# A two-layer trunk on one core: lone turns of the first attention and of the second layer's memory weights move next to other fp32 work, and the last output tile's end goes by halves

## The chip, the cores and the metric

The kernel runs on one core of one Trainium2 chip. Time is device time in microseconds (us) of one execution; a kernel's time is the median over its runs. TensorE (PE in the profile) does the matrix products, ScalarE (ACT) activations and copies with a scale, VectorE (DVE) elementwise work and reductions, GpSimd (POOL) a few fills, and SyncE (SP) issues nearly all DMA transfers.

## The reference

The reference is a trunk of two layers on x [1, 512, 1024] with 256 memory tokens. All values are fp32. Cut to what matters:

```python
def reference(x, mem, ...):
    for i in range(2):
        h = rms_norm(x, attn_norm[i])
        if i == 0:                       # differential attention, 6 heads
            proj = h @ w_in_diff[0]      # q, k, v, mem_q
            mix = diff_attention(q, k, v, ...)
        else:                            # gated linear attention, 4 heads
            proj = h @ w_in_gla[0]       # q, k, v, r, gate_low, mem_q
            mix = gla_attention(q, k, v, r, ...)
        cross = memory_cross_attention(mem_q, mem, ...)   # 4 heads, 256 tokens
        x = x + concatenate([mix, cross], -1) @ w_out[i]
        h = rms_norm(x, ffn_norm[i])
        x = x + conv_ffn(h, w_up[i], conv_w[i], conv_b[i], w_down[i])
    return x

def diff_attention(q, k, v, ...):        # d = 64, two maps m per head
    q = rms_norm(q, g[0]) * d ** -0.5
    k = rms_norm(k, g[1])
    p = softmax(q @ k.T + t5_bias, masked by 64-token chunks)
    w = p[map 0] - lam * p[map 1]
    return rms_norm(w @ v, out_norm_g) * (1 - lam_init)

def conv_ffn(h, w_up, conv_w, conv_b, w_down):            # DFF = 2816
    a, g = split(causal_depthwise_conv3(h @ w_up) + conv_b)
    return (silu(g) * a) @ w_down
```

## The kernel before

**Layout.** The stream x is held transposed, as eight tiles of 128 features by 512 tokens. Each product with a weight is done as three fp32r matmuls on halves of a number: high by high, high by low, low by high (lines 328 to 330 in `gemm`, 349 to 351 in `product`). The weights come in blocks of 512 KB on SyncE's queue into `raw` (three buffers); ScalarE rounds a block to `whi` (L251), VectorE makes the rest `wlo` (L254), and six buffers of each run ahead of TensorE.

**Two kinds of work on TensorE.** Besides the long runs of fp32r matmuls there are short fp32 ones: transposes (L218), logits (L733 in layer 0, L605 for the memory), values (L774, L643) and, in layer 1, the linear attention's products. They depend on ScalarE and VectorE and are strewn into the long runs by hand. A "lone turn" is a group of four transposes that stands alone between fp32r matmuls.

**The order written out by hand.** The strings `SCRIPT` (layer 0) and `GLA` (layer 1) are lists of words. A number takes that many microseconds of units (two contraction tiles of a gemm each) from the queue of fillers `F`; a letter calls a function with the number behind it. The letters of `SCRIPT` that matter here:

- `N` i: `norms`, the group norm of q (even i) or k (odd i) of head pair i // 2. ScalarE squares (L384, two instructions of 128x512), VectorE sums (L385), ScalarE does Ln and Exp (L239, L240), VectorE a Newton step (L225 to L227) and the scaling in place of `qs` or `ks` (L390, 128x1024).
- `P` h: `prepare`, the transposes of head h's `qs` and then `ks` on TensorE, each into a PSUM bank, which ScalarE copies out with a scale (L696).
- `L`, `M` t: `logits` of group t (with the banks lg or tp): matmuls (L733), bias and maximum on VectorE (L740), Exp on ScalarE (L743), weights on VectorE (L748 to L752).
- `T` t: `turn`, the transposes of the weights into a bank tp; ScalarE copies it out (L762).
- `V` t: `values` (L774); behind a head's last group come its Squares on ScalarE (L785).
- `s` h scales a head's output `o`, `F` h: `finish` transposes it and splits it into `xsh` (ScalarE, L308) and `xsl` (VectorE, L309).
- `a`, `b`: operands of the memory's gemms; `X` loads x again; `l`, `t`, `v`: logits, turn and values of the memory attention.

Layer 1's string has its own letters: `t` and `l` as above with `ma.turn` copying on VectorE (L630), `d`, `p`, `s`, `a`, `k`, `S`, `o`, `r`, `G`, `f` for the linear attention, `X` for the loads of x and the start of the output projection.

**What sets the order of the rest.** TensorE runs in the order in which the program calls it. The instructions of ScalarE and VectorE are put into one fixed order per engine when the program is built: a scheduler picks among those that it holds to be ready, by their place in the program, so a letter that moves in a string can move instructions on these engines too. On the chip each engine follows its own list and waits on semaphores of the others.

**PSUM.** Eight banks of 128x512 fp32 in four tags of two: mm (gemms), sm, lg, tp. The next use of a bank waits until its last reader is done.

**The tail.** The last feed-forward part adds a product's bank to two output tiles at a time. For the last one, n = 7, two half adds on VectorE (L1183) are followed each by a DMA to the output, one on SyncE's and one on ScalarE's queue (L1184).

Of the kernel before, what the change touches and what calls it, by code (L numbers as in the profile page):

```python
# [21 lines left out]
S = 512  # L22
# [14 lines left out]
VNAMES = ('v0', 'v0', 'v2')  # L37

SCRIPT = """
    17.75 P0 3.9  # L40
    L0 M1 a3 3.4 P1 5.05 a0 0.97
    1.94 a1 T0
    L2 M3 a2 3.57
    T1 4.86 N2 V0 T2 N3 V1 12.33
    L4 P2 4.55 P3 1.62 V2 T3 2.27 T4
    L5 M6 s0 V3 b1 2.6 V4 1.3 T5 1.3
    L7 M8 3.5 T6 F0 3.64 b0
    V5 T7 8.42 V6 s1 N5 N4 F1
    L9 V7 P4 b2 4.45 T8 T9 s2 3.0
    L10 V8 3.55 X P5 q0  # L50
    L11 b3 V9 T10 4.2
    L12 F2 V10 s3 T11 3.8 q1 k0
# [12 lines left out]
""", """  # L65
    l0 6.85 t0 t3
    l1
    d0 t2 1.55 t1 11.5 t5 14.85 t7 t4 7.15 p0 9.85 k0
    s0
    d1 S0 t6 a0 v0 v1 a1 S1 p1 o0 o1  # L70
    s1 r0 a2 k1
    d2 a3 p2 8.85 S2 0.75 o2 S3 G0 k2 o3 r1
    s2 a4 6.5 a5 S4 2.6 G1 S5
    d3 p3 o4 1.95 f0 0.65 o5 14.95 f1 r2
    s3 f2 a6 G2 1.95 k3 X 3.25 a7 0.65 S6 o6 1.0 f3 S7 o7 r3 13.25 G3 f4 f5
""")
K8 = tuple(range(KT))
C4 = tuple(range(4))
# [100 lines left out]
def trunk(ctx, tc, head_d, x_t, mem_t, wpack, cols_a_d, cols_d, conv_d, gate_d, rel_bias, diff_lambda, consts, onehot, out):  # L179
# [135 lines left out]
    def gemm(sh, sl, nb, key, w, evac, hook=None, late=False, spare=False):  # L315
        got, open_ = [], {}

        piece = [q[0] for q in plan].index(key)

        def unit(b, k0, k1):  # L320
            if not got:
                got.extend(weights(key, True))
            if k0 == 0:
                open_[b] = bank("tp" if spare and b == 0 else "lg" if late and b > 1 else "mm")[:, :w]
            p = open_[b]
            for k in range(k0, k1):
                hi, lo = got[k]
                mm(p, sh[k][:, blk(b)], hi, start=k == 0, stop=False)  # L328
                mm(p, sh[k][:, blk(b)], lo, start=False, stop=False)  # L329
                mm(p, sl[k][:, blk(b)], hi, start=False, stop=k == KT - 1)  # L330
                if b == nb - 1:
                    freed(piece, k)
            if k1 == KT:
                if hook is not None and b == 0:
                    hook()
                evac(b, open_.pop(b))
        units = [(b, k) for b in range(nb) for k in range(0, KT, 2)]
        if late:
            units.sort(key=lambda u: u[0] == nb - 1 or u[1] == KT - 2)
        for b, k in units:  # L340
            F.add(6 * w / 2370.0, lambda b=b, k=k: unit(b, k, k + 2))
# [84 lines left out]
    def token_rsqrt(tag, sq, nb, y, on_dve=False):  # L426
        p, ss = bank(tag), small("ss")[:, :nb]
        for b in range(nb):
            transpose(p[:, blk(b)], sq[:, blk(b)])
        V.reduce_sum(ss, p[:, :128 * nb].rearrange("p (b n) -> p b n", b=nb), axis=AX.X)  # L430
        return rsqrt(ss, nb, 1.0 / D, on_dve, y=y)
# [116 lines left out]
    def mem_kv(l):  # L548
        hs, ls = [None] * KT, [None] * KT
        km = [None]  # L550

        def operands(ks=range(KT)):
            if l == 0 and km[0] is None:
                mem_squares()
            if km[0] is None:
                km[0] = xtile().rearrange("p (b n) -> p b n", b=2)
            for k in ks:
                if k % 2 == 0:
                    mh, ml = split_tiles()
                c = blk(k % 2, 256)  # L560
                hs[k], ls[k] = mh[:, c], ml[:, c]
                split(hs[k], ls[k], memT[k // 2][:, c], c_mem(l, k))

        def ev(b, p):
            A.activation(km[0][:, b], p[:, :256], AF.Copy, scale=r_mem[:, b:b + 1])
            A.activation(vm[l][:, b], p[:, 256:], AF.Copy, scale=r_mem[:, b:b + 1])

        def keys(tag="lg"):
            F.need(f"kv{l}")
            p = bank(tag)  # L570
            for hp in range(2):
                for b in range(2):
                    transpose(p[:, 256 * hp + 128 * b:256 * hp + 128 * b + 128], km[0][:, b, blk(hp)])
            A.activation(kmT[l].rearrange("p a b -> p (a b)"), p, AF.Copy, scale=c_mk(l))
        gemm(hs, ls, 2, ("kv", l), 512, ev,
             (lambda: token_rsqrt("lg", mem_acc[0], 2, r_mem)) if l == 0 else None)
        F.add(0.0, lambda: group_norm(None, km[0], 2, 4, 64))
        F.mark(f"kv{l}")
        return operands, keys


    class MemAttn:
# [38 lines left out]
                V.tensor_mul(pv, pv, rc[:, blk(j, 2)].unsqueeze(2).to_broadcast([128, 2, 256]))  # L621
                self.live[2 * b + j] = pe

        def turn(self, u):
            pe = self.live[u]
            pt = bank("tp")
            for t in range(4):
                transpose(pt[:, blk(t)], pe[:, blk(t)])
            pT = xtile()
            (V.tensor_copy if self.l or u % 2 == 0 else A.copy)(pT, pt)  # L630
            self.live[u] = pT
# [27 lines left out]
    def diff_layer(pool, mix, acc):  # L659
# [28 lines left out]
        def prepare(h):  # L688
            pr, j = divmod(h, 2)
            t2 = []  # L690
            for src, g, nm in zip(qk[pr], (c_dq, c_dk), ("qT", "kT")):
                dst = pool.tile([128, S], F32, name=nm, bufs=3)
                p = bank("tp")
                for b in range(NB):
                    transpose(p[:, blk(b)], src[:, b, blk(j)])
                A.activation(dst, p, AF.Copy, scale=g)  # L696
                t2.append(dst)
            if j == 0:
                pairs[pr] = dict(s2=small("smd").rearrange("p (m b) -> p m b", b=8), nm=small("nmd"), rc=small("rcd"))
            heads[h] = dict(q=t2[0], k=t2[1], v=vs[pr], j=j, left=NB)  # L700
# [113 lines left out]
        for key in ORDER:  # L814
# [19 lines left out]
            "N": lambda i: norms(i // 2, i % 2), "a": lambda i: ops[0]((2 * i, 2 * i + 1)),  # L834
            "b": lambda i: ops[1]((2 * i, 2 * i + 1)), "k": lambda i: keys[i]("sm"),
            "q": lambda i: ma.queries() if i else (F.need("v2"), ma.norm()),
            "l": lambda i: ma.logits(i), "t": ma.turn, "v": lambda i: ma.values(i, "sm"),
            "s": lambda i: scales.pop(i)(), "X": lambda i: load_x(x_t),
            "O": lambda i: last.append(out_proj(0, mix, 1, acc, 5)), "!": lambda i: F.flush()}
        do(SCRIPT, doing)  # L840
# [4 lines left out]
    def gla_layer(pool, mix, acc):  # L845
# [203 lines left out]
        def finish(t):  # L1049
# [9 lines left out]
        do(GLA[1], {  # L1059
            "d": decays, "p": products, "s": scores, "a": lambda i: past_scores(i // 2, i % 2), "k": turn_keys,  # L1060
            "S": lambda i: states(i // 2, i % 2), "o": lambda i: outputs(i // 2, i % 2), "r": norm, "G": gate,
            "f": finish, "X": lambda i: (load_x(xres), out_proj(1, mix, 0, None)), "t": ma.turn, "l": lambda i: ma.logits(2 * i, 2 * i + 1),
            "v": lambda i: ma.values(i)})
        F.flush()

# [44 lines left out]
    def ffn(pool, l, acc):  # L1110
# [36 lines left out]
        for half, nq in enumerate(HALVES):  # L1147
            mids = []
            for q in range(base, base + nq):
                wa = weights(("ua", l, q))  # L1150
                wg = None
                for n in range(2):
                    ua = up(wa, n)
                    wg = wg or weights(("ug", l, q))
                    ug = up(wg, n)
                    if q == 0 and n == 0:
                        row_scales(acc[0])
                    ca = conv(*ua, 2 * q + n)
                    cg = conv(*ug, 22 + 2 * q + n)
                    A.activation(cg, cg, AF.Silu)  # L1160
                    V.tensor_mul(ca, ca, cg)
                    mh, ml = split_tiles() if len(mids) < 5 else split_tiles(pool, "mid", 18)
                    A.copy(mh, ca)
                    V.tensor_sub(ml, ca, mh.bitcast(F32))
                    mids.append((mh, ml))
            last = half == 1
            if last and l == 0:
                tables("natural_log_exp_and_others")
            acc2 = [None]
            for c in range(4):  # L1170
                if last and l == 0 and c == 0:
                    gw = gate_raw[0] = pool.tile([128, S], F32, name="cvo", bufs=6)[:96, :384]
                    G.memset(gw, 0.0)
                    for b in range(3):
                        load(gw[32 * b:32 * b + 17], gate_d)
                pn = bank("lg"), bank("tp")
                parts = weights(("dn", l, base, c))
                for n in range(2):
                    product(pn[n], parts, n, mids)
                for n in range(2):  # L1180
                    if last and l == 1 and c == 3 and n == 1:
                        for t, queue in ((blk(0, S // 2), nc.sync), (blk(1, S // 2), nc.scalar)):
                            V.tensor_add(xT[7][:, t], xT[7][:, t], pn[n][:, t])  # L1183
                            queue.dma_start(out[7, :, t], xT[7][:, t])  # L1184
                        continue
                    update(2 * c + n, pn[n], (lambda k: c_attn(1, k)) if last and l == 0 else None, acc2)
                    if last and l == 0:
                        nc.sync.dma_start(xres[2 * c + n], xT[2 * c + n])
                    if last and l == 1:
                        nc.sync.dma_start(out[2 * c + n], xT[2 * c + n])  # L1190
            base += nq
# [87 lines left out]
```

## Time and profile before

| | us |
|---|---|
| median of 3 runs (1164.59 to 1164.97) | 1164.59 |
| the profiled execution | 1164.66 |
| its span, first to last instruction | 1162.9 |
| TensorE busy, 5648 matmuls | 1158.3 |
| VectorE busy, 1261 instructions | 752.8 |
| ScalarE busy, 951 instructions | 544.9 |

The profile is one execution, taken by the hardware profiler. In a timeline a row gives the start, the length, the engine, the line of the program, the operation, its output and inputs, the shape and how many instructions are joined in the row; behind them may stand the engine's idle time in front of it and who ended it. Matmuls are pipelined: their own length (0.39 for 512 columns) is longer than the step from one to the next, so costs on TensorE are read from start to start. "PEclk" is the clock granted to TensorE, in tenths of full speed, in forty slices of the span.

The largest groups of the page are ScalarE's casts and VectorE's subtractions for the weights, 212 of each, and the fp32r matmuls of 512 columns:

| line, engine | what | count | busy us | mean ns |
|---|---|---|---|---|
| L251 ACT | `whi` from `raw` | 212 | 207.8 | 986 |
| L254 DVE | `wlo` from `raw`, `whi` | 212 | 240.5 | 1139 |
| L349 PE | products into mm | 438 | 171.6 | 392 |
| L328 PE | gemms into mm | 328 | 126.6 | 386 |

### The profile page before, as it was taken

Reading aid. Unit: us, or ns where it says so; the run is one execution under the profiler, and the core shown is the slowest. Engines: PE = TensorE matmul, PEld = TensorE weight load, DVE = VectorE, ACT = ScalarE, POOL = GpSimd, SP = SyncE. Lnnn points to the kernel's source line nnn. Section 1 sums busy time; section 2 is a strip of 40 time slices with the busy share of each in tenths; the row PEclk is TensorE's granted clock in tenths of the full one; section 3 lists DMA queues with packets and bytes.
Section 4 is the critical chain, followed back from the end, with each engine's and each line's share of the span. In section 5 each row is a group of like instructions: output and inputs, shape, how many; then the busy total and the mean of one; then the engine's idle time right before and its main releaser. Section 6 shows DMA issues by size and latency. Waiting matters only on the chain.

```text
span 1162.9 us, 14782 instructions
## 1 busy us (share of the span) xinstructions
PE 1158.3 (100%) x5648; PEld 965.8 (83%) x5648; DVE 752.8 (65%) x1261; ACT 544.9 (47%) x951; POOL 6.5 (1%) x30
## 2 busy tenths in 40 slices
PE   9999999999999999999999999999999999999998
PEld 7888887888888888888888888988888888888887
DVE  7676778688677326677457637867976733576741
ACT  6677686555344213344337634436544421344420
POOL 0000000000000000000000000000000000000000
PEclk9999999999999999999999999999999999999999
DMA  8522242233223223222342220332332323232231
GB/s 285 175 82 83 78 144 70 73 108 128 73 93 125 87 82 121 73 99 94 121 145 68 93 98 11 121 110 101 107 111 73 108 92 109 90 110 73 91 100 45
DMA packets 39652, 117.70 MB, mean 101 GB/s; under 512 B 4767, under 2 KB 7256, under 8 KB 39582
## 3 DMA queue, kind: packets, MB, share of 16 engines
q1 hardware_dynamic: 39150, 116.37, 29.5%
q8 instruction: 44, 0.72, 0.3%
q10 hardware_dynamic: 432, 0.39, 0.1%
q14 instruction: 26, 0.21, 0.1%
HBM read 112.54 MB, written 4.21 MB: 100 GB/s over the span
## 4 chain that ended last, share of the span: by engine, by line
PE 99%; DMA 0%; ACT 0%; DVE 0%; DVEq 0%; issue 0%
PE ps_mm L349 9%; PE ps_mm L350 9%; PE ps_mm L351 9%; PE ps_sm L351 8%; PE ps_sm L349 8%; PE ps_sm L350 8%; PE ps_mm L328 6%; PE ps_mm L330 6%; PE ps_mm L329 6%; PE ps_lg L349 3%; PE ps_tp L351 3%; PE ps_tp L349 3%; PE ps_lg L351 3%; PE ps_lg L350 3%; PE ps_tp L350 3%; PE ps_tp L218 3%
## 5 line engine op out<-in xcount | busy, mean ns | idle before, releaser
L251 ACT CAST whi<-raw 128x1024 fp32r<-128x1024 f32 (+4 forms) x212 | 207.8, 986 | 255.9 <-PE ps_tp L350 120.9
L254 DVE TENSOR_TENSOR wlo<-raw,whi 128x1024 fp32r<-128x1024 f32 (+4 forms) x212 | 240.5, 1139 | 116.3 <-ACT whi L251 115.5
L349 PE MATMUL ps_mm<-xsh,whi 128*128 128x512 f32 x438 | 171.6, 392 | 0.0
L350 PE MATMUL ps_mm<-xsl,whi 128*128 128x512 f32 x438 | 170.6, 389 | 0.0
L351 PE MATMUL ps_mm<-xsh,wlo 128*128 128x512 f32 x438 | 170.5, 389 | 0.0
L349 PE MATMUL ps_sm<-xsh,whi 128*128 128x512 f32 x378 | 147.0, 389 | 0.0
L350 PE MATMUL ps_sm<-xsl,whi 128*128 128x512 f32 x378 | 147.0, 389 | 0.0
L351 PE MATMUL ps_sm<-xsh,wlo 128*128 128x512 f32 x378 | 147.0, 389 | 0.0
L328 PE MATMUL ps_mm<-whi,xsh 128*128 128x512 f32 (+2 forms) x328 | 126.6, 386 | 0.0
L1127 ACT ACTIVATE cvo<-u,cv 128x512 f32<-128x512 f32 x88 | 71.4, 815 | 112.1 <-DVE u L1125 112.1
L330 PE MATMUL ps_mm<-whi,xsl 128*128 128x512 f32 (+2 forms) x328 | 123.0, 375 | 0.0
L329 PE MATMUL ps_mm<-wlo,xsh 128*128 128x512 f32 (+2 forms) x328 | 122.8, 374 | 0.0
L351 PEld LDWEIGHTS ps_mm<-xsh,wlo 128*128 128x128 f32 x438 | 82.2, 188 | 17.2
L350 PEld LDWEIGHTS ps_mm<-xsl,whi 128*128 128x128 f32 x438 | 82.3, 188 | 17.1 <-DVE xsl L309 0.4
L349 PEld LDWEIGHTS ps_mm<-xsh,whi 128*128 128x128 f32 x438 | 82.2, 188 | 17.0 <-issue 0.3
L1128 DVE SCALAR_TENSOR_TENSOR cvo<-u,cv,cvo 128x512 f32<-128x512 f32 x88 | 65.7, 748 | 36.2 <-ACT cvo L1127 36.0
L350 PEld LDWEIGHTS ps_sm<-xsl,whi 128*128 128x128 f32 x378 | 70.9, 188 | 14.7
L351 PEld LDWEIGHTS ps_sm<-xsh,wlo 128*128 128x128 f32 x378 | 70.9, 188 | 14.7
L349 PEld LDWEIGHTS ps_sm<-xsh,whi 128*128 128x128 f32 x378 | 70.9, 188 | 14.7
L330 PEld LDWEIGHTS ps_mm<-whi,xsl 128*128 128x128 f32 x328 | 61.7, 188 | 11.4
L328 PEld LDWEIGHTS ps_mm<-whi,xsh 128*128 128x128 f32 x328 | 61.7, 188 | 11.1 <-issue 0.7
L329 PEld LDWEIGHTS ps_mm<-wlo,xsh 128*128 128x128 f32 x328 | 61.8, 188 | 10.0
(309 smaller groups left out, 1777.7 us busy)
## 6 DMA issues: line engine op xcount, KB each, us to landing
raw<-in_wpack_dram SPq DMA_DIRECT2D x178, 512.0 KB, 3.4
xt<-in_x_t_dram SPq DMA_DIRECT2D x15, 256.0 KB, 5.6
raw<-in_wpack_dram SPq DMA_DIRECT2D x15, 256.0 KB, 5.5
raw<-in_wpack_dram SPq DMA_DIRECT2D x8, 384.0 KB, 3.6
xres<-xt SPq DMA_DIRECT2D x8, 256.0 KB, 3.0
xt<-xres SPq DMA_DIRECT2D x8, 256.0 KB, 5.2
out_dram<-xt SPq DMA_DIRECT2D x7, 256.0 KB, 2.0
bt<-bias_d SPq DMA_DIRECT2D x6, 256.0 KB, 4.7
```

The costliest lines, as they stand in the source:

```text
L218: nc.tensor.transpose(dst, src, ident[:n, :n])
L251: ins = A.copy(hi[:, c], raw[:, c])
L254: V.tensor_sub(lo[:, c], raw[:, c], hi[:, c].bitcast(F32))
L328: mm(p, sh[k][:, blk(b)], hi, start=k == 0, stop=False)
L329: mm(p, sh[k][:, blk(b)], lo, start=False, stop=False)
L330: mm(p, sl[k][:, blk(b)], hi, start=False, stop=k == KT - 1)
L349: mm(p, hi[:, blk(n)], bh, start=i == first, stop=False)
L350: mm(p, hi[:, blk(n)], bl, start=False, stop=False)
L351: mm(p, lo[:, blk(n)], bh, start=False, stop=i == last)
L1127: A.activation(c, u[:, 2:], AF.Identity, scale=cv[l][:, 2, j:j + 1], bias=cv[l][:, 3, j:j + 1])
L1128: V.scalar_tensor_tensor(c, u[:, 1:S + 1], cv[l][:, 1, j:j + 1], c, op0=ALU.mult, op1=ALU.add)
```

## The change

1. In `SCRIPT` turns 1, 2, 5, 6, 8 and 9 and the preparations of heads 1 and 3 stand next to other letters; numbers that they divided are joined. Head 1's preparation uses the banks sm instead of tp. The row scale of the memory (`token_rsqrt`), a hook inside the memory's first gemm before, is the letter `w` behind `V1`.
2. In `GLA` the memory's turns 2, 1, 5, 7 and 4 stand together behind 13.05 us of filler; 5 and 7 use the tag lg, 4 the tag sm. Near the end `a7` stands between `S6` and `o6`.
3. In the feed-forward's end the product for the last output tile stops two parts early. That much is added to the tile in one instruction; the last two parts are then done for 256 tokens at a time, into a bank of mm and one of sm, each followed by its add and its DMA.

```diff
@@ -37,16 +37,15 @@
 VNAMES = ('v0', 'v0', 'v2')
 
 SCRIPT = """
-    17.75 P0 3.9
-    L0 M1 a3 3.4 P1 5.05 a0 0.97
+    17.75 P0 P1 3.9
+    L0 M1 a3 8.45 a0 0.97
     1.94 a1 T0
-    L2 M3 a2 3.57
-    T1 4.86 N2 V0 T2 N3 V1 12.33
-    L4 P2 4.55 P3 1.62 V2 T3 2.27 T4
-    L5 M6 s0 V3 b1 2.6 V4 1.3 T5 1.3
-    L7 M8 3.5 T6 F0 3.64 b0
-    V5 T7 8.42 V6 s1 N5 N4 F1
-    L9 V7 P4 b2 4.45 T8 T9 s2 3.0
+    L2 M3 a2 8.43 N2 V0 T1 N3 2.6 T2 V1 w 9.73
+    P3 L4 P2 6.17 V2 T3 2.27 T4
+    L5 M6 s0 V3 b1 2.6 V4 T5 2.6
+    L7 M8 7.14 T6 F0 b0
+    V5 T7 8.42 T8 V6 s1 N5 N4 F1
+    L9 V7 P4 b2 4.45 s2 3.0 T9
     L10 V8 3.55 X P5 q0
     L11 b3 V9 T10 4.2
     L12 F2 V10 s3 T11 3.8 q1 k0
@@ -65,14 +64,14 @@
 """, """
     l0 6.85 t0 t3
     l1
-    d0 t2 1.55 t1 11.5 t5 14.85 t7 t4 7.15 p0 9.85 k0
+    d0 13.05 t2 t1 t5 t7 t4 22.0 p0 9.85 k0
     s0
     d1 S0 t6 a0 v0 v1 a1 S1 p1 o0 o1
     s1 r0 a2 k1
     d2 a3 p2 8.85 S2 0.75 o2 S3 G0 k2 o3 r1
     s2 a4 6.5 a5 S4 2.6 G1 S5
     d3 p3 o4 1.95 f0 0.65 o5 14.95 f1 r2
-    s3 f2 a6 G2 1.95 k3 X 3.25 a7 0.65 S6 o6 1.0 f3 S7 o7 r3 13.25 G3 f4 f5
+    s3 f2 a6 G2 1.95 k3 X 3.9 S6 a7 o6 1.0 f3 S7 o7 r3 13.25 G3 f4 f5
 """)
 K8 = tuple(range(KT))
 C4 = tuple(range(4))
@@ -572,8 +571,7 @@
                 for b in range(2):
                     transpose(p[:, 256 * hp + 128 * b:256 * hp + 128 * b + 128], km[0][:, b, blk(hp)])
             A.activation(kmT[l].rearrange("p a b -> p (a b)"), p, AF.Copy, scale=c_mk(l))
-        gemm(hs, ls, 2, ("kv", l), 512, ev,
-             (lambda: token_rsqrt("lg", mem_acc[0], 2, r_mem)) if l == 0 else None)
+        gemm(hs, ls, 2, ("kv", l), 512, ev)
         F.add(0.0, lambda: group_norm(None, km[0], 2, 4, 64))
         F.mark(f"kv{l}")
         return operands, keys
@@ -621,9 +619,9 @@
                 V.tensor_mul(pv, pv, rc[:, blk(j, 2)].unsqueeze(2).to_broadcast([128, 2, 256]))
                 self.live[2 * b + j] = pe
 
-        def turn(self, u):
+        def turn(self, u, tag="tp"):
             pe = self.live[u]
-            pt = bank("tp")
+            pt = bank(tag)
             for t in range(4):
                 transpose(pt[:, blk(t)], pe[:, blk(t)])
             pT = xtile()
@@ -688,9 +686,9 @@
         def prepare(h):
             pr, j = divmod(h, 2)
             t2 = []
-            for src, g, nm in zip(qk[pr], (c_dq, c_dk), ("qT", "kT")):
+            for src, g, nm, tag in zip(qk[pr], (c_dq, c_dk), ("qT", "kT"), {1: ('sm', 'sm')}.get(h, ("tp", "tp"))):
                 dst = pool.tile([128, S], F32, name=nm, bufs=3)
-                p = bank("tp")
+                p = bank(tag)
                 for b in range(NB):
                     transpose(p[:, blk(b)], src[:, b, blk(j)])
                 A.activation(dst, p, AF.Copy, scale=g)
@@ -834,7 +832,7 @@
             "N": lambda i: norms(i // 2, i % 2), "a": lambda i: ops[0]((2 * i, 2 * i + 1)),
             "b": lambda i: ops[1]((2 * i, 2 * i + 1)), "k": lambda i: keys[i]("sm"),
             "q": lambda i: ma.queries() if i else (F.need("v2"), ma.norm()),
-            "l": lambda i: ma.logits(i), "t": ma.turn, "v": lambda i: ma.values(i, "sm"),
+            "w": lambda i: token_rsqrt("lg", mem_acc[0], 2, r_mem), "l": lambda i: ma.logits(i), "t": ma.turn, "v": lambda i: ma.values(i, "sm"),
             "s": lambda i: scales.pop(i)(), "X": lambda i: load_x(x_t),
             "O": lambda i: last.append(out_proj(0, mix, 1, acc, 5)), "!": lambda i: F.flush()}
         do(SCRIPT, doing)
@@ -1059,7 +1057,8 @@
         do(GLA[1], {
             "d": decays, "p": products, "s": scores, "a": lambda i: past_scores(i // 2, i % 2), "k": turn_keys,
             "S": lambda i: states(i // 2, i % 2), "o": lambda i: outputs(i // 2, i % 2), "r": norm, "G": gate,
-            "f": finish, "X": lambda i: (load_x(xres), out_proj(1, mix, 0, None)), "t": ma.turn, "l": lambda i: ma.logits(2 * i, 2 * i + 1),
+            "f": finish, "X": lambda i: (load_x(xres), out_proj(1, mix, 0, None)),
+            "t": lambda u: ma.turn(u, {5: "lg", 7: "lg", 4: "sm"}.get(u, "tp")), "l": lambda i: ma.logits(2 * i, 2 * i + 1),
             "v": lambda i: ma.values(i)})
         F.flush()
 
@@ -1175,12 +1174,17 @@
                         load(gw[32 * b:32 * b + 17], gate_d)
                 pn = bank("lg"), bank("tp")
                 parts = weights(("dn", l, base, c))
+                final = last and l == 1 and c == 3
                 for n in range(2):
-                    product(pn[n], parts, n, mids)
+                    cut = len(parts) - 2 if final and n else len(parts)
+                    product(pn[n], parts[:cut], n, mids)
                 for n in range(2):
-                    if last and l == 1 and c == 3 and n == 1:
-                        for t, queue in ((blk(0, S // 2), nc.sync), (blk(1, S // 2), nc.scalar)):
-                            V.tensor_add(xT[7][:, t], xT[7][:, t], pn[n][:, t])
+                    if final and n == 1:
+                        V.tensor_add(xT[7], xT[7], pn[n])
+                        for t, tag, queue in ((blk(0, S // 2), "mm", nc.sync), (blk(1, S // 2), "sm", nc.scalar)):
+                            p = bank(tag)[:, :S // 2]
+                            product(p, parts[cut:], n, [(bh[:, t], bl[:, t]) for bh, bl in mids[cut:]])
+                            V.tensor_add(xT[7][:, t], xT[7][:, t], p)
                             queue.dma_start(out[7, :, t], xT[7][:, t])
                         continue
                     update(2 * c + n, pn[n], (lambda k: c_attn(1, k)) if last and l == 0 else None, acc2)
```

## The prediction

> **What bounds the kernel now.** I read the page first, then TensorE's waits, then the timeline where the diff touches the order.
>
> ```profile
> span 1162.9 us, 14782 instructions
> PE 1158.3 (100%) x5648; PEld 965.8 (83%) x5648; DVE 752.8 (65%) x1261; ACT 544.9 (47%) x951; POOL 6.5 (1%) x30
> PEclk9999999999999999999999999999999999999999
> PE 99%; DMA 0%; ACT 0%; DVE 0%; DVEq 0%; issue 0%
> PE ps_tp L454 <- PEq L1234: 0.8, 1, 0.8
> PE ps_mm L528 <- ACT xsh L308: 0.2, 1, 0.2
> ```
>
> TensorE is busy all through (first PE line), the chain that ended last is 99% TensorE (fourth line), and the waits of TensorE (the last two lines: total, times, longest) are 1.0 us, all at the start. So the end can come earlier only by fewer or cheaper matmuls or a shorter tail, and whatever makes TensorE wait is added to the end in full, for nothing later is slack that could absorb it. The clock stays full in every slice.
>
> The profiled execution took 1164.66 us (span 1162.9 and 1.8 around it), 0.07 above the median of 1164.59. I sum from 1164.66. A measurement of this kernel tells about 0.2% (2.3 us) from no change.
>
> **Part 1, the lone turns.** The price of a lone turn, in TensorE's timeline around turn 5:
>
> ```profile
> 117.21 0.40 PE L330 MATMUL ps_mm<-whi,xsl 128*128 128x512 f32 x1
> 117.45 0.60 PE L218 MATMUL ps_tp<-C,xt 128*128 128x128 f32 x4
> 117.81 0.48 PE L328 MATMUL ps_mm<-whi,xsh 128*128 128x512 f32 x1
> 118.12 0.39 PE L329 MATMUL ps_mm<-wlo,xsh 128*128 128x512 f32 x1
> 118.35 0.39 PE L330 MATMUL ps_mm<-whi,xsl 128*128 128x512 f32 x1
> ```
>
> From the matmul at 117.21 to that at 118.35 are 1.14 us. Undisturbed, three products at a pitch of 0.227 (118.12 to 118.35 is one such step) and four transposes at 0.109 (a quarter of the 0.44 from 143.71 to 144.14 below) make 1.117. Going out to fp32 work and back costs some 0.024 us. The written order drops from 51 such excursions to 42: six fewer in layer 0, three in the linear attention, and 9 × 0.024 = **-0.22 us**. The bounds are nothing and 0.3.
>
> **Part 2, turn 8 ahead of the norms.** Here the edit does more than move four transposes. Turn 8 goes from behind the 4.45 us of filler to directly before `V6 s1 N5 N4 F1`. Its copy out of PSUM runs on ScalarE, and in program order it now stands ahead of the Squares of N5 and N4, the norms of head pair 2. The built programs have ScalarE's instructions in this order (turn copies are line 762 before, 760 after; squares 384 and 383):
>
> ```
> before: copy xt<-ps_tp (T7) | Square xt<-ks x2 | Square xt<-qs x2 | Ln rs_y | v, qm | Exp | Ln | Exp | v, qm | xsh<-ps_tp (F1)
> after:  copy xt<-ps_tp (T7) | v, qm | v, qm | copy xt<-ps_tp (T8) | Square xt<-ks x2 | Square xt<-qs x2 | Ln | xsh<-ps_tp (F1) | Exp | Ln | Exp | Exp of L9
> ```
>
> Nothing in ScalarE's stream passes an earlier instruction, so the Squares now wait for the transposes of T8 on TensorE. In the timelines of before, ScalarE and VectorE did the norms right behind T7's copy:
>
> ```profile
> 131.50 0.58 ACT L762 COPY xt<-ps_tp 128x512 f32<-128x512 f32 x1
> 131.96 1.17 ACT L384 ACTIVATE xt<-ks 128x512 f32<-128x512 f32 x2
> 133.01 1.16 ACT L384 ACTIVATE xt<-qs 128x512 f32<-128x512 f32 x2
> 135.57 0.21 ACT L240 ACTIVATE rs_y<-rs_y 128x16 f32<-128x16 f32 x1
> 141.75 0.69 ACT L308 ACTIVATE xsh<-ps_tp,cols 128x512 fp32r<-128x512 f32 x1 [1.85 <-PE ps_tp L218]
> ```
> ```profile
> 135.93 1.23 DVE L390 TENSOR_TENSOR ks<-ks,rs_y 128x1024 f32<-128x1024 f32 x1
> 137.49 1.23 DVE L390 TENSOR_TENSOR qs<-qs,rs_y 128x1024 f32<-128x1024 f32 x1
> 142.48 0.75 DVE L309 SCALAR_TENSOR_TENSOR xsl<-ps_tp,cols,xsh 128x512 fp32r<-128x512 f32 x1 [3.77 <-ACT xsh L308]
> 143.14 0.68 DVE L740 CUSTOM_DVE_ANT_0 xt<-ps_lg,bt 128x512 f32<-128x512 f32 x1
> ```
>
> qs was scaled by 138.72, and TensorE's transposes of qs (the letter P4) came five microseconds later, at 143.71:
>
> ```profile
> 140.23 1.05 PE L774 MATMUL ps_sm<-vv,xt 128*128 128x128 f32 x8
> 141.12 0.60 PE L218 MATMUL ps_tp<-C,o 128*128 128x128 f32 x4
> 143.71 0.60 PE L218 MATMUL ps_tp<-C,qs 128*128 128x128 f32 x4
> 144.14 0.60 PE L218 MATMUL ps_tp<-C,ks 128*128 128x128 f32 x4
> ```
>
> In the changed kernel T8 leaves its old place behind the filler and starts where V6 did, at 140.23. All else follows from there.
> - TensorE gets to P4 0.44 (T8's four transposes) + 3.48 (140.23 to 143.71) = 3.92 us after T8's start.
> - T8's copy starts 0.63 after T8, as F1's evacuation did (141.12 to 141.75).
> - From the copy's start to the end of the scaling of qs took 138.72 - 131.50 = 7.22 us behind T7. The chain is the same (four Squares, reductions, two Ln and Exp, Newton steps, ks, qs), so 7.22 is the part that I trust.
> - VectorE has more in that stretch than before. Its built order puts F1's xsl (0.75) and both bias operations of L9 (0.68 each) ahead of the scaling of qs. Back to back they step some 0.66 (142.48 to 143.14); a part of them falls into VectorE's waits for ScalarE. In full they are 2.1, at the least nothing. Following the two orders instruction by instruction I get 1.4 and take that.
> - TensorE therefore waits 0.63 + 7.22 + 1.4 - 3.92 = **5.3 us**, and I take 5.4 with a tenth for the semaphore to TensorE. The bounds are 3.9 (nothing inserted) and 6.2 (all in full, plus a reciprocal).
>
> Queued behind the waiting transposes is everything else of TensorE: the keys' transposes, the memory operands, the filler and all that follows. ScalarE and VectorE use the wait to catch up with casts and L9's softmax, so I expect no second stall from it.
>
> [...]
>
> **Part 3, other moves in layer 0.** T6, F0, V5 and T7 now stand directly behind each other, and T7 reuses the PSUM bank that T6's copy empties. Before, the timelines of TensorE and ScalarE had
>
> ```profile
> 124.18 0.60 PE L218 MATMUL ps_tp<-C,xt 128*128 128x128 f32 x4
> 124.76 0.63 PE L218 MATMUL ps_tp<-C,o 128*128 128x128 f32 x4
> ...
> 129.33 1.05 PE L774 MATMUL ps_sm<-vv,xt 128*128 128x128 f32 x8
> 130.22 0.60 PE L218 MATMUL ps_tp<-C,xt 128*128 128x128 f32 x4
> ```
> ```profile
> 129.04 1.04 ACT L251 CAST whi<-raw 128x1024 fp32r<-128x1024 f32 x1
> ...
> 130.34 0.47 ACT L673 ACTIVATE ks<-ps_mm,r_x 128x256 f32<-128x256 f32 x1
> ```
>
> T6 now begins 0.44 (itself) + 0.44 (F0) + 0.89 (V5, 129.33 to 130.22) ahead of T7's 130.22, at 128.45, so its copy could start at 129.1 and end at 129.7. But the built order has the evacuations of qs and ks ahead of it, which ran until 130.81 behind a cast (129.04) that now moves ahead too. Copy done between 129.7 and 131.4 means a wait of T7 between 0 and 1.1 us; I take 0.2: before, T6's copy and F0's split stood ahead of that cast, so it can start about a microsecond earlier than it did. The same move removes a pause of about 0.15 that F0 had behind T6 (124.18 to 124.76 are 0.58 instead of 0.44). Together **+0.05**. P1 directly behind P0 uses the two sm banks, empty there; P3, T1, T5 and the memory scale move by a few microseconds among fillers that cover them. All these I cost at nothing; if one cover fails, its price is a copy of 0.6.
>
> **Part 4, the second layer's turns.** t2, t1, t5, t7, t4 stand together where t1 was:
>
> ```profile
> 653.50 0.68 DVE L621 TENSOR_TENSOR xt<-xt,rcm 128x512 f32<-128x512 f32 x1
> 662.73 0.60 PE L218 MATMUL ps_tp<-C,xt 128*128 128x128 f32 x4
> ```
>
> The last softmax product ends at 654.18, over 8 us before; five banks in three tags take the five turns, so none waits for a copy. VectorE gets five copies of 0.68 at once, and a weight split behind them is late by some 3 us against a lead of more than that. Nothing, beyond part 1.
>
> **Part 5, the tail.** The end of before, in the timeline:
>
> ```profile
> 1158.88 0.39 PE L351 MATMUL ps_tp<-midh,wlo 128*128 128x512 f32 x1
> 1159.31 0.75 DVE L1183 TENSOR_TENSOR xt<-xt,ps_tp 128x256 f32<-128x256 f32 x2 [6.11 <-PE ps_tp L351]
> 1159.75 0.33 SPq L1184 DMA_DIRECT2D out_dram<-xt  x1
> 1160.09 0.35 ACTq L1184 DMA_DIRECT2D out_dram<-xt  x1
> ```
>
> Two half adds followed the last matmul, the second 0.34 behind the first. Six matmuls of 512 columns become twelve of 256, whose step is 0.12 (nine from 732.17 to 733.13):
>
> ```profile
> 732.17 0.28 PE L329 MATMUL ps_mm<-wlo,xsh 128*128 128x256 f32 x1
> ...
> 733.13 0.28 PE L328 MATMUL ps_mm<-whi,xsh 128*128 128x256 f32 x1
> ```
>
> That is 12 × 0.12 - 6 × 0.227 = +0.08 on TensorE. Only one half add is then left behind the last matmul, and the full add lies under the matmuls: -0.34. **-0.26 us**, between -0.4 and +0.1.
>
> **The sum.** 1164.66 - 0.22 + 5.4 + 0.05 - 0.26 = 1169.63, so **1169.6 us**.
>
> **The rivals.**
>
> *The clock falls in the stall.* At the start of the program, with TensorE cold, the timeline has
>
> ```profile
> 5.43 1.05 PE L528 MATMUL ps_sm<-whi,xsh 128*128 128x512 f32 x2
> 6.28 0.66 PE L528 MATMUL ps_mm<-wlo,xsh 128*128 128x512 f32 x2
> ```
>
> Two matmuls take 0.85 from 5.43 to 6.28, 0.427 each instead of 0.227, and full rate comes at 6.28, some 5.5 us after TensorE's first instruction at 0.8. If 5.4 us of idling put it back there, the restart costs 5.5 × (1 - 0.227/0.427) = 2.6 us, giving 1172.2. For it: idling before the start did bring half rate. Against it: TensorE never pauses longer than 0.2 later on, so nothing shows how long a pause is needed. [...] It is a close rival.
>
> *The norms are ready in time.* If the scaling of qs ends before TensorE reaches P4, at about 144.15 (140.23 + 3.92), the kernel is faster: 1164.66 - 0.22 - 0.26 = 1164.2, no measurable change. It decides at a chain of 3.3 us (3.92 - 0.63) from the start of T8's copy to the scaled qs. Before, the four Squares alone took 2.2 (131.96 to 134.17) and the scaling of qs 1.23, in series 3.4 without a reduction, an Ln or a Newton step, so it needs a chip that does Squares ahead of the copy that stands before them.
>
> *More waits.* T7 behind T6's copy at its full 1.1, or a cast that is late after the stall by a copy or two, adds 0.6 to 1.5: about 1170.7.
>
> **How the numbers follow.** Stall without a fall of the clock 0.46; with it 0.42; norms in time 0.05; further waits 0.07. The likeliest is 1169.6, its own range 1168.1 to 1170.5 from the bounds 3.9 and 6.2. The clock's case reaches from 1170.7 (a shorter stall) to 1173.6; I cut it at 1173.1, for a range of 1168.0 to 1173.1. Faster by over 0.2% needs 2.3 us, and all gains together are 0.5: 0.01. Within 0.2% is the in-time case, 0.05. Slower is the rest, 0.94.
>
> **What would show it.** Right: TensorE waits once, about 5 us, on VectorE's scaling of qs (its line 389 there), at about 144 us; the Squares start behind T8's copy at about 141.4; the last add is a single 256-column one; nine fewer excursions. A clock slice below 9 behind 144, and matmuls at 0.427, would show the rival. Wrong: no wait in front of P4, squares at 132, or a longer wait somewhere else.

## The result: 1171.92 us, and the profile after

| | before | changed |
|---|---|---|
| median us (6 runs each) | 1164.57 | 1171.92 |
| range us | 1163.94 to 1164.97 | 1171.22 to 1172.44 |
| profiled execution, span us | 1162.9 | 1170.2 |
| mean granted clock of that execution | 1.000 | 0.997 |

The ratio is 1.0063, with a 95% interval of 1.0052 to 1.0074: the changed kernel is slower by 7.3 us. The median lies 2.3 above the predicted 1169.6, inside the range, and next to the 1172.2 of the rival in which the clock falls.

The head of the page of the changed kernel, and its waits of TensorE (total, times, longest; up to the tail, lines of the program stand one or two lower in this kernel than in the kernel before):

```profile
span 1170.2 us, 14797 instructions
...
PEclk9999989999999999999999999999999999999999
```
```profile
PE ps_tp L217 <- DVE rcd L746: 5.3, 1, 5.3
PE ps_tp L453 <- PEq L1238: 0.8, 1, 0.8
PE ps_tp L217 <- ACT qT L694: 0.2, 1, 0.2
PE ps_mm L527 <- DVE whi L489: 0.2, 1, 0.2
```

One new wait of 5.3 us, before transposes, on VectorE; a small one on ScalarE (the 0.8 and the other 0.2 are at the start, as before); and one slice of the clock, the sixth, below 9. The releaser "rcd L746" has to be read with care: it is the instruction on VectorE right behind the one that matters, the scaling of qs. TensorE's timeline there:

```profile
140.34 0.60 PE L217 MATMUL ps_tp<-C,xt 128*128 128x128 f32 x4
...
143.26 1.16 PE L772 MATMUL ps_sm<-vv,xt 128*128 128x128 f32 x8
149.67 1.09 PE L217 MATMUL ps_tp<-C,qs 128*128 128x128 f32 x4 [5.25 <-DVE rcd L746]
150.55 1.06 PE L217 MATMUL ps_tp<-C,ks 128*128 128x128 f32 x4
151.26 0.78 PE L327 MATMUL ps_mm<-whi,xsh 128*128 128x512 f32 x1
151.83 0.63 PE L328 MATMUL ps_mm<-wlo,xsh 128*128 128x512 f32 x1
152.26 0.63 PE L329 MATMUL ps_mm<-whi,xsl 128*128 128x512 f32 x1
...
154.39 0.41 PE L328 MATMUL ps_mm<-wlo,xsh 128*128 128x512 f32 x1
154.65 0.40 PE L329 MATMUL ps_mm<-whi,xsl 128*128 128x512 f32 x1
154.88 0.40 PE L327 MATMUL ps_mm<-whi,xsh 128*128 128x512 f32 x1
```

T8 starts at 140.34, P4 at 149.67 where 144.26 was due (3.92 behind T8, as forecast). Behind the wait four transposes take 0.88 instead of 0.44 (149.67 to 150.55) and matmuls of 512 columns step 0.43 (151.83 to 152.26) instead of 0.23 (154.65 to 154.88), until about 154.4: half rate for 4.7 us. ScalarE's and VectorE's timelines in the same stretch:

```profile
140.97 0.58 ACT L760 COPY xt<-ps_tp 128x512 f32<-128x512 f32 x1 [0.96 <-PE ps_tp L217]
141.45 1.15 ACT L383 ACTIVATE xt<-ks 128x512 f32<-128x512 f32 x2
142.50 1.14 ACT L383 ACTIVATE xt<-qs 128x512 f32<-128x512 f32 x2
```
```profile
144.66 0.74 DVE L308 SCALAR_TENSOR_TENSOR xsl<-ps_tp,cols,xsh 128x512 fp32r<-128x512 f32 x1
145.65 0.68 DVE L738 CUSTOM_DVE_ANT_0 xt<-ps_lg,bt 128x512 f32<-128x512 f32 x1
146.26 1.22 DVE L389 TENSOR_TENSOR ks<-ks,rs_y 128x1024 f32<-128x1024 f32 x1
147.48 0.68 DVE L738 CUSTOM_DVE_ANT_0 xt<-ps_lg,bt 128x512 f32<-128x512 f32 x1
148.29 1.23 DVE L389 TENSOR_TENSOR qs<-qs,rs_y 128x1024 f32<-128x1024 f32 x1
```

ScalarE idles for 0.96 in front of T8's copy although ks and qs have long been there, and does the four Squares only behind it, from 141.45 instead of 131.96. The chain from the copy to the scaled qs runs from 140.97 to 149.52, 8.55 us; P4 starts 0.15 later.

The 0.2 us on `qT` is P2's. P3 now stands directly in front of L4 and P2, and P2 waits until ScalarE has copied P3's banks; that copy stood behind a cast of a weight block that waited for its load:

```profile
94.64 1.05 ACT L250 CAST whi<-raw 128x1024 fp32r<-128x1024 f32 x1 [1.39 <-DMA raw<-in_wpack_dram]
...
96.03 0.67 ACT L694 ACTIVATE qT<-ps_tp,cols 128x512 f32<-128x512 f32 x1
```

The tail, in the timeline of the changed kernel:

```profile
1166.74 0.28 PE L350 MATMUL ps_sm<-midh,wlo 128*128 128x256 f32 x1
...
1167.06 0.42 DVE L1187 TENSOR_TENSOR xt<-xt,ps_sm 128x256 f32<-128x256 f32 x1 [0.21 <-PE ps_sm L350]
1167.51 0.35 ACTq L1188 DMA_DIRECT2D out_dram<-xt  x1
```

The last DMA goes out 0.77 behind the start of the last matmul instead of 1.21.

**Where the 7.3 us came from.** The last matmul starts at 1166.74 instead of 1158.88, 7.86 later. The wait is 5.41 of it: P4 starts 6.41 behind V7 (143.26 to 149.67), where e1 below, with the same order on TensorE, takes 1.00; 5.25 of this is idle. The half rate is about 4.7 × (1 - 0.227/0.427) = 2.2 by this estimate, and the rows agree: from P4 to the third matmul of L328 behind it are 4.72 (149.67 to 154.39), in e1's trace 2.50 (143.97 to 146.47). The rest is 0.2: P2's and T7's pauses and the tail's longer matmuls, less a shorter pause at F0, the lone turns and a start that happened to be 0.3 earlier. Behind the last matmul 0.5 is won back: 7.86 - 0.5 is the 7.3 between the spans.

### The profile page after: what moved, and what is told of

Its sections match the earlier page's. It is cut to its first block, busy times and chain, and to the rows that moved or that the text cites. A ratio compares the mean times of both kernels' runs of the same rounds, so it can differ in the third digit from the quotient of the medians.

```text
span 1170.2 us, 14797 instructions
## 1 busy us (share of the span) xinstructions
PE 1160.5 (99%) x5654; PEld 967.8 (83%) x5654; DVE 752.1 (64%) x1262; ACT 545.3 (47%) x951; POOL 6.5 (1%) x30
## 4 chain that ended last, share of the span: by engine, by line
PE 95%; ACT 2%; DVE 1%; DMA 1%; issue 0%; ACTq 0%
PE ps_mm L348 9%; PE ps_mm L349 9%; PE ps_mm L350 9%; PE ps_sm L350 7%; PE ps_sm L348 7%; PE ps_sm L349 7%; PE ps_mm L327 5%; PE ps_mm L329 5%; PE ps_mm L328 5%; PE ps_lg L348 3%; PE ps_lg L350 3%; PE ps_lg L349 3%; PE ps_tp L348 3%; PE ps_tp L350 3%; PE ps_tp L349 3%; PE ps_tp L217 2%
## 5 line engine op out<-in xcount | busy, mean ns | idle before, releaser
L328 PE MATMUL ps_mm<-wlo,xsh 128*128 128x512 f32 (+2 forms) x328 | 123.3, 376 | 0.0
L328 PEld LDWEIGHTS ps_mm<-wlo,xsh 128*128 128x128 f32 x328 | 62.2, 190 | 10.4
```

## The experiments

The theory: the loss is P4's wait for the norms, because T8's copy is late on ScalarE, and the clock that falls in the wait. The rivals: the loss sits in the other moves, or the mere place of the copy costs. How long a wait it takes for the clock to fall was open.

**e1, the norms called ahead of T8.**

```diff
-    V5 T7 8.42 T8 V6 s1 N5 N4 F1
+    V5 T7 N5 N4 8.42 T8 V6 s1 F1
```

> The changed kernel with N5 and N4 called directly behind T7, so that ScalarE's built order has the four Squares ahead of T8's copy again; TensorE's order is that of the changed kernel to the last instruction. Theory (the whole loss is the wait of P4 for the norms, and the fall of the clock behind it): no wait before P4, clock 1.000, time 1171.9 - 5.25 - 2.6 = 1164.1 us. Rival (the new order on TensorE itself, the GLA turns or the banks cost something): a wait of some us stays somewhere, and the time is above 1166.

Measured 1164.83 us over 11 runs, ratio 1.0002 (0.9993 to 1.0011). TensorE waits only at the start, and P4 follows V7 without a pause:

```profile
142.97 1.16 PE L772 MATMUL ps_sm<-vv,xt 128*128 128x128 f32 x8
143.97 0.60 PE L217 MATMUL ps_tp<-C,qs 128*128 128x128 f32 x4
```

With TensorE's order untouched, two words put elsewhere in the string take away the whole loss. So it came from the order on ScalarE and VectorE; the GLA turns, the banks and the merged turns cost nothing that the times can tell.

**e2, T8 alone in the kernel before.**

```diff
-    V5 T7 8.42 V6 s1 N5 N4 F1
-    L9 V7 P4 b2 4.45 T8 T9 s2 3.0
+    V5 T7 8.42 T8 V6 s1 N5 N4 F1
+    L9 V7 P4 b2 4.45 T9 s2 3.0
```

> The kernel before with nothing but T8 moved in front of V6. Theory: a single wait of 5.2 to 5.4 us before P4, the clock falls, 1164.6 + 5.3 + 2.6 = 1172.5 us. Rival (the loss needs the other moves too): under 1167 us.

Measured 1171.88 us (5 runs, ratio 1.0072, 1.0058 to 1.0086), with one wait of 5.25 us in its profile and a clock below 1.000 in each run. One word makes the loss. Two of the five runs took 1174.4 and 1174.6; what added 2.6 there stays open. Single runs of kernels without the wait stand as far out (1166.57 in e1, 1166.44 in e8).

**e4 and e3, T8 earlier by one and by two filler units.** The number 8.42 is divided around T8.

```diff
-    V5 T7 8.42 T8 V6 s1 N5 N4 F1
+    V5 T7 7.12 T8 1.3 V6 s1 N5 N4 F1       # e4
+    V5 T7 5.83 T8 2.59 V6 s1 N5 N4 F1      # e3
```

> The changed kernel with T8 one filler unit (1.36 us on TensorE) earlier, so that its copy releases the norms earlier. Theory: the wait shrinks by the same 1.36 to 3.9 us. [...]

> The changed kernel with T8 two filler units (2.7 us) earlier. Theory: the wait is 2.5 us or somewhat less, since the keys' scaling then stands ahead of the inserted work on VectorE. [...]

Measured: e4 1170.73 us, e3 1169.07 us (5 runs each; ratios 1.0051 and 1.0037). The waits before P4 in e4 and in e3:

```profile
PE ps_tp L217 <- DVE rcd L746: 4.2, 1, 4.2
```
```profile
PE ps_tp L217 <- DVE rcd L746: 3.3, 1, 3.3
```

The wait shrinks as T8 moves up, but by 1.1 and 2.0, not by 1.36 and 2.7. In e4 two evacuations of v and qm hold the copy on ScalarE: it starts 3.38 ahead of V7 (140.12 to 143.50) instead of 2.29 (140.97 to 143.26), and that 1.09 is what the wait lost. In e3 the copy leads by 5.06, 2.8 more than in the changed kernel, but F1's split, whose xsh waits 0.40 for TensorE itself, and L9's bias operations stand ahead of the scaling of qs. The clock is below 1.000 in all 5 runs of e4 and in 3 of 5 of e3 (how far such a count can be trusted stands in the last section).

**e7 and e9, the keys' norm alone ahead of T8** (e9 with T8 one unit earlier besides).

```diff
-    V5 T7 8.42 T8 V6 s1 N5 N4 F1
+    V5 T7 N5 8.42 T8 V6 s1 N4 F1           # e7
+    V5 T7 N5 7.12 T8 1.3 V6 s1 N4 F1       # e9
```

> The changed kernel with only N5, the keys' norm, called behind T7; N4, the queries' norm, stays behind T8's copy. Theory (the wait is the length of the chain from T8's copy to the scaled qs): two Squares and one scaling of 1.23 leave the chain, 1.05 + 1.2 and a Newton step, so the wait is 5.25 - 2.65 = 2.6 us. [...]

> e7 with T8 one filler unit earlier besides. Theory: as between the changed kernel and e4, the copy comes 0.85 us earlier (two evacuations of v and qm stand ahead of it), and the wait is 2.6 - 0.85 = 1.75 us. [...]

e7 took 1168.83 us (5 runs, ratio 1.0036), its wait is the expected 2.6 (the view names an instruction near the scaling of qs again, the reciprocal L781). e9 took 1169.00 us (7 runs, ratio 1.0030, 1.0018 to 1.0041), and its wait missed the expected 1.75. TensorE's timelines of e7 and of e9:

```profile
144.15 1.16 PE L772 MATMUL ps_sm<-vv,xt 128*128 128x128 f32 x8
147.91 1.08 PE L217 MATMUL ps_tp<-C,qs 128*128 128x128 f32 x4 [2.60 <-DVE rs L781]
```
```profile
143.70 1.16 PE L772 MATMUL ps_sm<-vv,xt 128*128 128x128 f32 x8
147.32 1.09 PE L217 MATMUL ps_tp<-C,qs 128*128 128x128 f32 x4 [2.46 <-DVE rs L781]
...
150.34 0.47 PE L327 MATMUL ps_mm<-whi,xsh 128*128 128x512 f32 x1
150.65 0.40 PE L328 MATMUL ps_mm<-wlo,xsh 128*128 128x512 f32 x1
```

In e9 the copy leads V7 by 1.1 more than in e7, but VectorE's list has F1's xsl and L9's bias operations ahead of the scaling of qs; F1's transposes are on TensorE at 142.10, 1.6 ahead of V7, in any case, and the wait shrank by 0.14 only. The clock was below 1.000 in 4 of 5 runs of e7 and in 4 of 7 of e9. The times show it too: e9's runs at clock 1.000 took 1167.0 to 1167.5, those at 0.999 took 1169.0 to 1169.9. In e9's profile half rate lasted 3.4 us and ended at about 150.5 (stretches in the last section), so the clock fell at about 147.1, when TensorE had idled for some 2.2 us (since 147.32 - 2.46 = 144.86).

**e6, T8 directly behind T7.**

```diff
-            pt = bank("tp")
+            pt = bank("lg" if t == 8 else "tp")
-    V5 T7 8.42 T8 V6 s1 N5 N4 F1
+    V5 T7 T8 8.42 V6 s1 N5 N4 F1
```

> The changed kernel with T8 directly behind T7 (into a bank lg, since the next tp bank is still read by F0's split). On ScalarE T8's copy still stands ahead of all four Squares. Theory (the copy costs because it is late, not because of its place): no wait before P4, clock 1.000, 1164.4 to 1165 us. Rival (the mere place of the copy ahead of the Squares, or the extra evacuation, costs): a wait before P4 stays.

Measured 1164.37 us (10 runs, ratio 0.9999, 0.9990 to 1.0009); no wait before P4. ScalarE's timeline has T8's copy ahead of all four Squares, as in the changed kernel, but nine microseconds earlier:

```profile
131.23 0.58 ACT L760 COPY xt<-ps_tp 128x512 f32<-128x512 f32 x1
131.70 0.59 ACT L760 COPY xt<-ps_lg 128x512 f32<-128x512 f32 x1
132.18 1.17 ACT L383 ACTIVATE xt<-ks 128x512 f32<-128x512 f32 x2
```

The place in ScalarE's list costs 0.47; the lateness of what it waits for cost the rest.

**e5, the tail alone in the kernel before** (the third part of the change, unaltered).

> The kernel before with nothing but the new tail. Theory: TensorE 0.08 us longer, the last DMA starts 0.77 us behind the start of the last matmul instead of 1.21; together -0.26 to -0.4 us, about 1164.0 us against 1164.3 of the kernel before, within what the times can tell, so it is read in the trace. Rival (the end of the output DMA sets the end, and the second queue is hidden anyway): the last instruction ends as long behind the last matmul as before.

Measured 1164.36 against 1164.45 us, ratio 1.0000 (0.9991 to 1.0009). The end of its timeline, the last matmul and the last DMA:

```profile
1159.82 0.28 PE L351 MATMUL ps_sm<-midh,wlo 128*128 128x256 f32 x1
...
1160.59 0.35 ACTq L1189 DMA_DIRECT2D out_dram<-xt  x1
```

From the start of the last matmul to the end of the span are 3.5 us (1159.82 to 1163.3), before 4.0 (1158.88 to 1162.9). The twelve half matmuls start the last one 0.19 later than six whole ones (11 × 0.12 against 5 × 0.227). That leaves some 0.3 of gain, seen in the trace and too small for the times.

**e8, e1 with P3 put back.**

```diff
-    P3 L4 P2 6.17 V2 T3 2.27 T4
+    L4 P2 4.55 P3 1.62 V2 T3 2.27 T4
-    V5 T7 8.42 T8 V6 s1 N5 N4 F1
+    V5 T7 N5 N4 8.42 T8 V6 s1 F1
```

> The version with all gains and none of the losses found: e1 with P3 put back to its old place (the transposes of head 2 waited for ScalarE's copy of head 3's, 0.2 to 0.4 us of the changed kernel). Theory: no wait of TensorE behind the start, 1164.6 - 0.2 (lone turns) + 0.1 (T7) - 0.3 (tail) = 1164.2 us, not told from the kernel before by the times. Rival (the lone turns cost more than 0.024 us each): under 1163.

Measured 1164.36 us (11 runs, ratio 0.9998, 0.9989 to 1.0007), TensorE waits only at the start. With every loss found in the times taken out, the moves gain nothing that the times can tell. No version that was run beats the kernel before.

## Why the prediction was right, and where its likeliest case was wrong

- *What bounds the kernel.* Right: a wait in the middle comes out at the end, in the changed kernel and in e2, e4, e3, e7 and e9.
- *The wait* (part 2 of the prediction). 5.4 us were said, 5.41 measured from start to start (5.25 of idling); the copy 0.63 behind T8 as forecast, the chain 8.55 for 7.22 + 1.4 = 8.62, and 0.15 (149.52 to 149.67) for the tenth allowed behind it for the semaphore, an allowance that no row of before shows by itself. The inserted VectorE work stands where the forecast has it: xsl and the two bias operations lie between 144.66 and 148.1. T8 at 140.34 for 140.23 is in part luck: a start 0.3 earlier hides most of what the other moves cost ahead of it. e1, e2 and e6 show that the cause is the one named, the Squares behind a copy that is late. That ScalarE keeps its list agrees with the 0.96 of idling ahead of T8's copy at 140.97, while the Squares' inputs had been there since 129.8 (the last evacuation of ks, 129.32 and 0.46 long).
- *The clock: the step that failed is the ranking of the cases.* The stall without a fall got 0.46, the one with it 0.42; the fall happened in all 6 runs of the changed kernel and all 5 of e2. The range held the result because it took that case in; the likeliest time missed by the price of the fall. That price was said to be 2.6 us, from 5.5 us of half rate at the start; it was 2.2, from 4.7 us behind the wait. With 2.6 the sum would have been 1172.2 for the measured 1171.9, in part by luck: the moves of layer 0 (below) were said too low by about as much. The odds were the author's estimate: before had no wait of TensorE over 0.8 us, that one at its start, so no run had shown how long a pause it takes. The runs decide it: a wait of 2.46 us went with a fall in e9's profile, and one of 4.15 (e4) goes with a clock below 1.000 in 5 of 5 runs.
- *The lone turns* (-0.22). Too small for the times: e8 is within 0.1% of the kernel before. The changed order on TensorE has the nine fewer excursions, but no run sets their gain apart; the 0.024 each is a reading of one turn in the kernel before.
- *The other moves of layer 0* (+0.05). Too low by about 0.5: from P0 to T8 the changed kernel takes 93.54 (46.80 to 140.34) and the one before, for the same work, 93.12 (47.11 to 140.23), where +0.05 and six lone turns less made it 0.1 shorter. P3 and P2 cost 0.3 to 0.4 where nothing was said, because P3's copy stood behind a cast that waited 1.39 for its load: from L4 to P2 are 1.38 (95.38 to 96.76), before 1.06, in e8, which puts P3 back, 1.06 again. It is not always as long: e1, with P3 in the new place, has 1.23. V5 to T7 took 1.15 (129.15 to 130.30) instead of 0.89, a pause of 0.26 for 0.2 said.
- *The second layer's turns* (nothing). Right: no wait of TensorE there in any profile.
- *The tail* (-0.26). Right in kind and size: -0.3 in e5's trace, no difference in its times.
- *The rivals.* "Norms in time" needed a chain of 3.3 us; it was 8.55. The same version with the norms called earlier (e1) gives what that rival said, no measurable change.

## What to carry to other kernels

Where one engine's order is written by hand and the others' follows from it, a moved instruction takes its consumers along: look in the lists of the other engines for what now stands behind the moved instruction's copy, and for who waits for that. Moving work beside other work of its kind was forecast at 0.02 us a time and shows in no time here; one copy that came nine microseconds later on ScalarE cost 7. And cost a stall of TensorE with the clock: here waits of 2.46 and 5.25 us cost 1.5 and 2.2 us more in half rate behind them (1.5 in e9, whose 147.32 to 151.35 stands for 143.97 to 146.47 in e1; 2.2 in the changed kernel), and e3's wait of 3.27 none in its profile (148.12 to 150.65 for the same rows).

## What the runs showed of the hardware

In these profiles the length of a pause of TensorE alone does not settle whether its clock falls. The profiles that show a fall have waits of 2.46 (e9), 2.60 (e7, by its steps of 0.43 behind the wait, 150.06 to 150.49), 4.15 (e4) and 5.25 us (the changed kernel, e2); the one profile with a wait and without a fall, e3's, waited 3.27, at a granted clock of 1.00 from 144 to 156. Clock below 1.000 in 4 of 7, 4 of 5, 3 of 5 (e3), 5 of 5 and 11 of 11 runs, in order of the wait. A single 0.999 does not prove a fall in the wait: kernels without any such wait (before, e1, e5, e6, e8) show it in 11 of 96 runs. So e3's three (1169.07 to 1169.75 us, the other two 1168.45 and 1168.47) are the least sure. TensorE's clock in e9, by stretches (start and end, length, busy time and count, granted clock, DMA share, GB/s):

```profile
143.00:146.00 3.00, 1.85 (x16) 1.00 0.01 3
146.00:149.00 3.00, 1.68 (x9) 0.68 0.28 87
149.00:152.00 3.00, 3.00 (x12) 0.75 0.00 0
152.00:155.00 3.00, 3.00 (x14) 1.00 0.00 0
```

The clock falls inside the second stretch, at about 147.1 (2 × 0.32 × 3 = 1.9 ahead of 149.00) and so ahead of the next matmul at 147.32, and is back in the third: half rate lasted 2 × (0.32 + 0.25) × 3 = 3.4 us. In the changed kernel the stretches around the wait are

```profile
144.00:150.00 6.00, 0.75 (x6) 0.80 0.09 27
150.00:156.00 6.00, 6.00 (x22) 0.63 0.06 18
```

where 0.80 and 0.63 make 2 × (0.20 + 0.37) × 6 = 6.8 us of half rate. It began at about 147.6 (2 × 0.20 × 6 = 2.4 ahead of 150.00), when TensorE had idled for 3.2 us (since 149.67 - 5.25 = 144.42). In e2 it began sooner in a wait of the same length:

```profile
144.00:150.00 6.00, 0.75 (x6) 0.69 0.09 28
150.00:156.00 6.00, 6.00 (x25) 0.75 0.05 17
```

Half rate to the end of the first stretch makes 2 × 0.31 × 6 = 3.7 us, so the clock fell at about 146.3, when TensorE had idled for 1.9 us (since 149.60 - 5.25 = 144.35). In e4 it fell later: 0.96 from 144 to 150 puts it at about 149.5, behind the whole wait of 4.15 us (148.81 - 4.15 = 144.66 to 148.81). So 1.9 us of idling came before a fall in one profile, and 3.27 before none in another, one profile for each; what decides besides the length of a wait is not shown, nor how short a wait is safe. None under 2.46 us was tried in this place.

P0, the first work behind the opening gemm, starts at 46.80 in the profile of the changed kernel and at 47.88 in e5's, with the same work ahead of it. Such a difference is about as large as the scatter between the runs of one kernel, and may be a part of it; with one profile for each kernel this is not shown.
